# First input chunks loaded straight into a resident buffer, index scores that yield twice, and a norm's sums by operand, in a decoder trunk on one core

## The chip, the cores and the metric

The kernel runs on one core of one Trainium2 chip. The metric is the time of one execution in microseconds on the device, the median of several runs. Five engines of the core work side by side, each through its own list of instructions in order: TensorE (PE in the profile) for matmuls and transposes, VectorE (DVE), ScalarE (ACT), GpSimd (POOL), and SyncE (SP), which here only issues transfers. PEld is the loading of weights into TensorE's array, which overlaps its matmuls. Transfers between HBM and the on-chip memory go through DMA engines; an engine's row with a q behind its name (SPq, POOLq) is that engine issuing one.

## The reference

A trunk of two layers over 1024 tokens of width 1024, all in float32. Cut to what matters:

```python
for i in range(2):
    a = rmsnorm(h, norm_mix_pre[i])
    q, k, v, qi, ki, wi, u_conv, u_pool = split(a @ w_in[i])
    # partial rotary on q, k, qi, ki
    # dsa_sparse_attention, per block of 128 tokens:
    #   idx = sum over 16 index heads of relu(qi . ki) * wi; the top 256 causal keys are kept
    #   softmax attention of 8 heads over these keys
    mix = concatenate([attention, conformer_conv(u_conv), multiscale_pool(u_pool)])
    h = h + rmsnorm(mix @ w_out[i], norm_mix_post[i])
    m = square(relu(rmsnorm(h, norm_mlp_pre[i]) @ w_up[i])) @ w_down[i]
    h = h + rmsnorm(m, norm_mlp_post[i])
    h = h + sigmoid(h @ ple_gate[i]) * (p[i] @ ple_proj[i])
# rmsnorm(x, g) = x / sqrt(mean(x^2) + 1e-6) * g
```

## The kernel before

The tokens are cut in two halves of 512. A tensor is kept transposed, features on the 128 partitions and 512 tokens along them, so a half of width 1024 is eight chunks of 128 x 512. Every dense product is a chain of *units*: a unit takes one block of 128 output features, eight input chunks, and three matmuls for each of them (L252, L257, L258), because each number is split into a rounded high part and a low remainder and the product low times low is left out. That is 24 matmuls of 128 x 512 into one bank `pd` of a ring of three. `prepare` (L205) loads a unit's weights (512 KB, L208, issued by SP into a ring of two buffers `wraw`), rounds them on ScalarE (`whi`, L213) and subtracts on GpSimd (`wlo`, L214). The input chunks are split likewise by `split_g`: ScalarE L274 rounds, VectorE L275 subtracts; the two parts lie in a ring of 16 `slots`.

An RMS norm runs in three steps. `Sq.add` squares each chunk on ScalarE (L290) and adds it up on VectorE (L294); the last square is kept apart, so a norm has two operands. `token_sums` multiplies them with a column of ones (L307), so that four columns hold the sums of 4 x 128 tokens. `rms` scales them (VectorE L318), takes the power -1/2 (GpSimd L320), and `spread` brings the result back along the partitions (L312). In the input projection the norm's factor `rb` (ScalarE L327) is multiplied in as the units are evacuated.

The work goes in eight phases: the input projection (`win`) and the rest (`m`) of each layer and half, in the order of PHASES. A `win` phase has 21 units: six for the conv and pooling groups, and 15 for attention, among them I0 to I7, the index queries, whose results `put` rounds (L269), subtracts (L270) and writes to HBM (`qiS`, L364), and V, whose blocks are transposed by TensorE (L451). The first half's input is loaded by `first_x` ahead of everything, the second half's by a second call that is made at the 16th unit of the first phase. A chunk of x is loaded into a buffer `dtmp` (L1053), split, squared, and the buffer is given back. The ring `dtmp` has nine buffers, and almost every step between a bank and HBM uses it. `yT`, a resident 8 x 128 x 1024 buffer, holds the trunk's state between phases; until the first `m` phase nothing is in it.

The conv, pooling and attention stages are generators that run beside the dense units: `run` gives them a budget for each unit of the phase, and `advance` takes one step of the first generator in the list that has one. A generator that yields None passes the turn to the next. `attention` first scores index queries against keys (`index`: `load_k`, then for each block and four heads `load_q`, issued by GpSimd into a ring of two `qst`, L617, then L610, relu L651, sum L655), then selects, then does softmax and the weighted sum (transposes L798, products L806 and L807). What is left of an attention when its `m` phase begins is drained alone. Program order is only the start: a scheduler then reorders the instructions of each engine by its own estimate of times, and the rings decide who waits.

Of the kernel before, what the change touches and what calls it, by code (L numbers as in the profile page):

```python
# [16 lines left out]
OP = mybir.AluOpType  # L17

P = 128
# [4 lines left out]
NK = D // P  # L24
# [62 lines left out]
def tile_trunk(ctx: ExitStack, tc: tile.TileContext, xT, pT, pos, vecs, invf, cinv,  # L87
               win, wout, wup, wdown, wgate, wple, wcp, outT):
    nc = tc.nc
    te, ve, sc, gp, sy = nc.tensor, nc.vector, nc.scalar, nc.gpsimd, nc.sync  # L90
# [22 lines left out]
    qiS = dram.tile([2, 1024, S], F32, name="qiS")  # L113
# [12 lines left out]
    dtmp = Ring("dtmp", 9, [P, HALF])  # L126
# [10 lines left out]
    yT = const.tile([P, NK, HALF], F32, name="yT")  # L137
# [4 lines left out]
    def tiny(name, n=4, dt=F32, bufs=4):  # L142

        key = name + side[0][0]
        if key not in tinies:
            tinies[key] = [small.tile([P, n], dt, name=f"{key}{i}") for i in range(bufs)]
        tinies[key].append(tinies[key].pop(0))
        return tinies[key][-1]
# [11 lines left out]
    ones = const.tile([P, 1], F32, name="ones")  # L160
# [44 lines left out]
    def prepare(src):  # L205
        n = src.shape[1] // 4
        raw = wraw.get()
        sy.dma_start(raw[:, :4 * n], src)  # L208
        parts = []
        for i in range(n):  # L210
            hi, lo = whi.get(), wlo.get()
            r = raw[:, 4 * i:4 * i + 4]
            sc.activation(hi, r, AF.Copy)  # L213
            gp.tensor_tensor(lo, r, hi.bitcast(F32), op=OP.subtract)  # L214
            parts.append((hi, lo))
        wraw.put(raw)
        return parts
# [54 lines left out]
    def split_g(hi, lo, src, g):  # L272

        sc.activation(hi, src, AF.Identity, scale=g)  # L274
        ve.scalar_tensor_tensor(lo, src, g, hi.bitcast(F32), op0=OP.mult, op1=OP.subtract)  # L275


    class Sq:
# [20 lines left out]
        def rms(self, ps, other=None):  # L299
            rms(ps, self.acc, D, 1e-6, other)  # L300
            dtmp.put(*self.acc)

    def token_sums(ps, srcs):

        for j in range(4):
            for i, src in enumerate(srcs):
                te.matmul(ps[:, j:j + 1], src[:, j * P:(j + 1) * P], ones, start=i == 0, stop=i == len(srcs) - 1)  # L307

    def spread(ps, t4):

        for j in range(4):
            te.transpose(ps[:, j * P:(j + 1) * P], t4[:, j:j + 1].to_broadcast([P, P]), ident)  # L312

    def rms(ps, srcs, n, eps, other=None):

        token_sums(other or ps, srcs)
        v = tiny("rv")
        ve.tensor_scalar(v, (other or ps)[:, :4], 1.0 / n, eps, op0=OP.mult, op1=OP.add)  # L318
        r = tiny("rr")
        gp.tensor_tensor(r, v, mhalf, op=OP.pow)  # L320
        spread(ps, r)
# [146 lines left out]
    def conv_pool(l, hf, yc):  # L468
# [98 lines left out]
        ve.tensor_tensor(sq[0], sq[0], sq[1], op=OP.add)  # L567
        ctmp.put(sq.pop())
        rms(ps, sq, 256, 1e-5)
        ctmp.put(*sq)  # L570
        xs = []
# [24 lines left out]
    def attention(l, hf):  # L596
        blocks = list(range(4 * hf, 4 * hf + 4))
        sel = [b for b in blocks if (b + 1) * P > TOPK]
# [4 lines left out]
        def scores(q, W, k0):  # L603

            out = []
            for n0 in range(0, W, 512):
                n1 = min(W, n0 + 512)
                ps = banks.get()
                for k in range(2):
                    te.matmul(ps[:, :n1 - n0], q, kd[:, k, k0 + n0:k0 + n1], start=k == 0, stop=k == 1)  # L610
                out.append((n0, n1, ps))
            return out

        def load_q(src, b, h0, nh):
            x = qst.get()
            v = src.rearrange("k (d h) t -> (k d) h t", h=nh)
            gp.dma_start(x, v[:, h0:h0 + 4, b * P:(b + 1) * P])  # L617
            return x

        def load_k(h, k0, n):  # L620
            for dup in range(2):
                sy.dma_start(kd[dup * 64:(dup + 1) * 64, :, k0:k0 + n].bitcast(F32),
                             kS[l, :, :, :n].rearrange("k (d h) t -> h d k t", h=3)[h])
# [16 lines left out]
        def index():  # L640

            load_k(2, 0, Ws[-1])
            for j, b in enumerate(sel):
                W = Ws[j]
                for h in range(16):
                    if h % 4 == 0:
                        q = load_q(qiS, b, h, 16)
                    w = wiT[:, l, b, h:h + 1]
                    for n0, n1, ps in scores(q[:, h % 4], W, 0):
                        r, at = ps[:, :n1 - n0], idx[j][:, n0:n1]  # L650
                        sc.activation(r, r, AF.Relu)  # L651
                        if h == 0:
                            sc.activation(at, r, AF.Copy, scale=w)
                        else:
                            ve.scalar_tensor_tensor(at, r, w, at, op0=OP.mult, op1=OP.add)  # L655
                        banks.put(ps)
                    if h % 4 == 3:
                        qst.put(q)
                    yield W * 1.32 / 1024
                gp.affine_select(idx[j][:, W - P:], idx[j][:, W - P:], pattern=[[-1, P]], compare_op=OP.is_ge,  # L660
                                 fill=LOW, base=0, channel_multiplier=1)
            state["index", l, hf] = True
# [161 lines left out]
        def attend(some, at, ring):  # L824
# [3 lines left out]
            for step in [(kv, b, g) for kv in range(2) for b in some for g in (0, 2)] + [None]:  # L828
# [21 lines left out]
                before = step, pr  # L850

        yield from index()
        if hf == 0:
            while ("q", l, hf) not in state:
# [192 lines left out]
    def first_x(hf):  # L1047
        ts = slice(hf * HALF, hf * HALF + HALF)
        sq = Sq()
        xs = []  # L1050
        for k in range(NK):
            h = dtmp.get()
            sy.dma_start(h, xT[k * P:(k + 1) * P, ts])  # L1053
            if k == 0 and hf == 0:
                ready.append(prepare(coming.pop(0)))
            x = slots.get()
            xs.append(x)
            split_g(x[:, 0], x[:, 1], h, vec[:, 0, V_MIX_PRE + k:V_MIX_PRE + k + 1])
            sq.add(h)
            dtmp.put(h)  # L1060
        return xs, sq


# [31 lines left out]
    def drain(l, hf):  # L1095

        while advance([x for x in bg if x[0] == (l, hf)]) is not None:
            pass

    state["x", 0, 0] = first_x(0)  # L1100
    for i, (l, hf, phase) in enumerate(PHASES):
        if phase == "win":
            extra = {}
            if i == 0:
                extra = {2: lambda: (sy.dma_start(fr, invf), rope_tables(0)), 5: lambda: rope_tables(1),
                         16: lambda: state.update({("x", 0, 1): first_x(1)})}
            run(win_phase(l, hf, *state["x", l, hf]), RATES[i], extra)
        else:
            drain(l, hf)
            run(m_phase(l, hf), RATES[i])  # L1110
# [62 lines left out]
```

## Time and profile before

| | us |
|---|---|
| median of 3 runs | 2802.93 (2802.38 to 2804.43) |
| the profiled execution | 2803.82 |
| its span, first to last instruction | 2802.1 |
| TensorE busy | 2701.1 (96%) |
| VectorE busy | 1698.4 (61%) |
| ScalarE busy | 1599.7 (57%) |
| GpSimd busy | 1372.7 (49%) |

All times of rows are microseconds from the start of the span unless marked ns. The granted clock (PEclk) is the TensorE clock that the throttle granted, as a share of full speed: 1.00 is 2.4 GHz and 0.50 is 1.2 GHz. In rows of waits "A <- B" says that A's engine was idle until B was done; DMA stands for a transfer.

### The profile page before, as it was taken

The page shows a single profiled execution, that of the slowest core. Times are in us where ns is not written, and L with a number is a line of the kernel's source. Part 1 is how long each engine was busy: PE and PEld are TensorE (multiplying, and loading weights), DVE is VectorE, ACT ScalarE, POOL GpSimd, SP SyncE. Part 2 cuts the span into 40 slices and gives each one's busy share as a digit, 9 for nine tenths or more (in the row PEclk, how much of TensorE's full clock was granted, in tenths as well). Part 3 has the DMA queues.
Part 4 walks back from the last instruction along what each step waited for, and adds up shares of the span by engine and source line. Part 5 has one row for each costly group of instructions (what it writes and reads, how often), then busy time and mean ns, then how long its engine had stood idle before and what let it go on. Part 6 is the DMA issues. An engine that isn't in the chain of part 4 may idle for free.

```text
span 2802.1 us, 37352 instructions
## 1 busy us (share of the span) xinstructions
PE 2701.1 (96%) x12512; PEld 2224.5 (79%) x12512; DVE 1698.4 (61%) x3399; ACT 1599.7 (57%) x3008; POOL 1372.7 (49%) x1085
## 2 busy tenths in 40 slices
PE   8889989999999999999999989999999999999998
PEld 6678877887888787788888778788878887788886
DVE  7869668678657868784422595676785561411123
ACT  5357668776766544685633434677757664533343
POOL 4655425444334674544344764444443346544446
PEclk9999999999999999999999999999999999999999
DMA  5677555432343566543333656533222354422223
GB/s 177 203 184 226 147 140 150 109 98 84 94 109 108 185 204 192 177 128 117 90 101 103 213 156 212 155 105 110 93 85 84 105 176 150 144 98 98 98 94 132
DMA packets 193425, 380.63 MB, mean 136 GB/s; under 512 B 17232, under 2 KB 76752, under 8 KB 193232
## 3 DMA queue, kind: packets, MB, share of 16 engines
q1 hardware_dynamic: 150992, 357.26, 39.8%
q0 software_dynamic: 42240, 20.98, 4.4%
q8 instruction: 99, 1.62, 0.2%
q14 instruction: 94, 0.77, 0.1%
HBM read 305.81 MB, written 72.35 MB: 135 GB/s over the span
## 4 chain that ended last, share of the span: by engine, by line
PE 78%; DVE 10%; DMA 5%; issue 2%; ACT 2%; POOL 1%; SPq 0%; POOLq 0%; ACTq 0%; DVEq 0%
PE pd L252 22%; PE pd L257 22%; PE pd L258 22%; PE bank L610 6%; PE bank L798 2%; DVE bank L549 2%; PE bank L807 1%; PE bank L806 1%; DMA wraw<-win 1%; DVE row L761 1%; DVE dtmp L884 1%; PE pd L255 1%; PE pd L307 1%; POOL wlo L214 1%; DVE dtmp L270 1%
## 5 line engine op out<-in xcount | busy, mean ns | idle before, releaser
L214 POOL TENSOR_TENSOR wlo<-wraw,whi 128x512 fp32r<-128x512 f32 x824 | 1097.4, 1336 | 1215.7 <-ACT whi L213 1147.0
L252 PE MATMUL pd<-slot,whi 128*128 128x512 f32 x3296 | 1305.6, 397 | 44.5 <-ACT whi L213 8.9
L258 PE MATMUL pd<-slot,wlo 128*128 128x512 f32 x3168 | 1245.4, 394 | 5.4 <-POOL wlo L214 5.1
L257 PE MATMUL pd<-slot,whi 128*128 128x512 f32 x3168 | 1245.8, 393 | 0.0
L213 ACT ACTIVATE whi<-wraw 128x512 fp32r<-128x512 f32 x824 | 512.8, 627 | 722.3 <-PE pd L257 520.2
L252 PEld LDWEIGHTS pd<-slot,whi 128*128 128x128 f32 x3296 | 625.1, 190 | 181.6 <-ACT whi L213 10.8
L258 PEld LDWEIGHTS pd<-slot,wlo 128*128 128x128 f32 x3168 | 600.1, 189 | 132.6 <-POOL wlo L214 9.2
L257 PEld LDWEIGHTS pd<-slot,whi 128*128 128x128 f32 x3168 | 600.6, 190 | 121.0 <-DVE slot L275 1.2
L610 PE MATMUL bank<-kd,qst 128*128 128x512 f32 (+3 forms) x1024 | 263.4, 361 | 15.6 <-DMA qst<-qiS 6.3
L655 DVE SCALAR_TENSOR_TENSOR idx<-bank,wiT,idx 128x512 f32<-128x512 f32 (+3 forms) x300 | 190.0, 652 | 89.1 <-ACT bank L651 80.8
L610 PEld LDWEIGHTS bank<-kd,qst 128*128 128x128 f32 x1024 | 181.2, 193 | 50.5 <-DMA qst<-qiS 7.2
L651 ACT ACTIVATE bank<-bank 128x512 f32<-128x512 f32 (+2 forms) x320 | 154.6, 506 | 71.5 <-PE bank L610 69.5
L1004 DVE TENSOR_TENSOR yT<-yT,pd 128x512 f32<-128x512 f32 x96 | 65.5, 684 | 203.7 <-PE pd L258 203.1
L990 DVE SCALAR_TENSOR_TENSOR pd<-pd,rb 128x512 f32<-128x512 f32 x112 | 78.0, 696 | 166.9 <-PE pd L258 166.6
L678 DVE TENSOR_SCALAR_CACHE_REDUCE row<-row,cc 128x640 f32<-128x640 uint16 (+1 forms) x124 | 133.5, 1078 | 63.4 <-ACT row L692 56.6
L549 DVE SCALAR_TENSOR_TENSOR bank<-win,vec,bank 128x512 f32<-128x512 f32 x232 | 165.5, 746 | 7.7 <-ACT bank L547 6.0
L776 DVE CUSTOM_DVE_ANT_0 row<-bank,idx 128x512 f32<-128x512 f32 (+3 forms) x160 | 91.7, 592 | 71.4 <-PE bank L610 50.4
L692 ACT ACTIVATE row<-row,cc 128x768 f32<-128x768 uint16 (+1 forms) x124 | 121.4, 982 | 22.9 <-DVE cc L698 20.5
L270 DVE TENSOR_TENSOR cmat<-bank,cmat 128x512 fp32r<-128x512 f32 (+1 forms) x160 | 98.3, 631 | 34.5 <-ACT cmat L269 30.9
L270 DVE TENSOR_TENSOR slot<-pd,slot 128x512 fp32r<-128x512 f32 x112 | 76.8, 687 | 52.8 <-ACT slot L269 52.5
L784 ACT ACTIVATE row<-row,nmc 128x384 f32<-128x384 f32 (+5 forms) x96 | 84.1, 877 | 36.0 <-DVE nmc L780 26.7
L269 ACT ACTIVATE cmat<-bank 128x512 fp32r<-128x512 f32 (+1 forms) x160 | 83.7, 546 | 26.4 <-PE bank L798 23.1
(216 smaller groups left out, 2724.1 us busy)
## 6 DMA issues: line engine op xcount, KB each, us to landing
wraw<-wup SPq DMA_DIRECT2D x128, 512.0 KB
wraw<-wdown SPq DMA_DIRECT2D x128, 512.0 KB
wraw<-win SPq DMA_DIRECT2D x84, 512.0 KB
qiS<-dtmp SPq DMA_DIRECT2D x64, 256.0 KB
slot<-mixS SPq DMA_DIRECT2D x32, 512.0 KB
wraw<-wgate SPq DMA_DIRECT2D x32, 512.0 KB
qst<-qiS POOLq DMA_DIRECT2D x48, 256.0 KB, 3.9
hS<-yT SPq DMA_DIRECT2D x48, 256.0 KB
```

The costliest lines, as they stand in the source:

```text
L213: sc.activation(hi, r, AF.Copy)
L214: gp.tensor_tensor(lo, r, hi.bitcast(F32), op=OP.subtract)
L252: te.matmul(ps, wh, xh, start=i == 0, stop=False)
L257: te.matmul(ps, wh, xl, start=False, stop=False)
L258: te.matmul(ps, wl, xh, start=False, stop=i == n - 1)
L270: ve.tensor_tensor(lo, src, hi.bitcast(F32), op=OP.subtract)
L549: ve.scalar_tensor_tensor(acc[:, c] if k == TAPS - 1 else pa, src, w, pa, op0=OP.mult, op1=OP.add)
L610: te.matmul(ps[:, :n1 - n0], q, kd[:, k, k0 + n0:k0 + n1], start=k == 0, stop=k == 1)
L651: sc.activation(r, r, AF.Relu)
L655: ve.scalar_tensor_tensor(at, r, w, at, op0=OP.mult, op1=OP.add)
L678: ve.tensor_scalar(flags[:, :Ws[j]], of[j], t, None, op0=op, op1=OP.add, accum_out=dst[:, j:j + 1])
L692: sc.activation(flags[:, :Ws[j]], of[j], AF.Sign, scale=-1.0, bias=c[:, j:j + 1], accum_out=cnt[:, j:j + 1])
```

## The change

There are three parts.

*The chunks of x.* `first_x` loads the eight chunks of a half straight into `yT[:, k]`, all ahead of the splits; splits and squares read yT, and no `dtmp` is taken for x. The first unit's weights are loaded behind the second chunk instead of the first.

*The index stage.* `index` issues the load of its first index queries and then yields None twice, ahead of any score.

*The norm's sums.* `token_sums` puts the sums of operand i into columns 4i to 4i + 3, each of them a matmul that starts and stops its own accumulation, one operand after the other. `rms` adds the second four columns by one more VectorE instruction where there are two operands.

```diff
     def token_sums(ps, srcs):

-        for j in range(4):
-            for i, src in enumerate(srcs):
-                te.matmul(ps[:, j:j + 1], src[:, j * P:(j + 1) * P], ones, start=i == 0, stop=i == len(srcs) - 1)
+        for i, src in enumerate(srcs):
+            for j in range(4):
+                te.matmul(ps[:, 4 * i + j:4 * i + j + 1], src[:, j * P:(j + 1) * P], ones, start=True, stop=True)
...
         token_sums(other or ps, srcs)
-        v = tiny("rv")
-        ve.tensor_scalar(v, (other or ps)[:, :4], 1.0 / n, eps, op0=OP.mult, op1=OP.add)
+        v, sums = tiny("rv"), other or ps
+        ve.tensor_scalar(v, sums[:, :4], 1.0 / n, eps, op0=OP.mult, op1=OP.add)
+        if len(srcs) == 2:
+            ve.scalar_tensor_tensor(v, sums[:, 4:8], 1.0 / n, v, op0=OP.mult, op1=OP.add)
         r = tiny("rr")
...
         def index():

             load_k(2, 0, Ws[-1])
+            first = load_q(qiS, sel[0], 0, 16)
+            for _ in range(2):
+                yield None
             for j, b in enumerate(sel):
                 W = Ws[j]
                 for h in range(16):
                     if h % 4 == 0:
-                        q = load_q(qiS, b, h, 16)
+                        q = first if j == h == 0 else load_q(qiS, b, h, 16)
...
         for k in range(NK):
-            h = dtmp.get()
+            h = yT[:, k]
             sy.dma_start(h, xT[k * P:(k + 1) * P, ts])
-            if k == 0 and hf == 0:
+            if k == 1 and hf == 0:
                 ready.append(prepare(coming.pop(0)))
+        for k in range(NK):
+            h = yT[:, k]
             x = slots.get()
             xs.append(x)
             split_g(x[:, 0], x[:, 1], h, vec[:, 0, V_MIX_PRE + k:V_MIX_PRE + k + 1])
             sq.add(h)
-            dtmp.put(h)
         return xs, sq
```

The numbers of instructions on TensorE, ScalarE, GpSimd and SyncE stay as they are; VectorE has twelve more, one for each norm with two operands. Line numbers grow by two to six. Three places show how the order moves.

On SyncE, the part of the list where the last index queries (qiS) of the first phase are written. Before, with the second half's loads of x (xT) among the writes:

```order
L208 DMA wraw_92<-win 128x1024
L1053 DMA dtmp_106<-xT 128x512
L364 DMA qiS<-dtmp_103 128x512
L364 DMA qiS<-dtmp_102 128x512
L1053 DMA dtmp_102<-xT 128x512
L208 DMA wraw_91<-win 128x1024
L364 DMA qiS<-dtmp_107 128x512
L364 DMA qiS<-dtmp_101 128x512
L1053 DMA dtmp_101<-xT 128x512
```

And now the same writes:

```order
L208 DMA wraw_92<-win 128x1024
L366 DMA qiS<-dtmp_102 128x512
L366 DMA qiS<-dtmp_101 128x512
L208 DMA wraw_91<-win 128x1024
L366 DMA qiS<-dtmp_107 128x512
L366 DMA qiS<-dtmp_103 128x512
L208 DMA wraw_92<-win 128x1024
L366 DMA qiS<-dtmp_104 128x512
```

All sixteen loads of x have moved to the first fifteen rows of this engine; between the writes only weights are left.

On ScalarE, the rows that end with the first norm's factor (rb). Before:

```order
L290 ACTIVATE dtmp_108<-dtmp_109 128x512
L213 ACTIVATE whi_95<-wraw_92 128x512
L213 ACTIVATE whi_94<-wraw_91 128x512
L213 ACTIVATE whi_96<-wraw_92 128x512
L197 ACT_TABLE_LOAD
L197 ACTIVATE dtmp_105<-dtmp_101 128x512
L199 ACTIVATE dtmp_104<-dtmp_101 128x512
L327 ACTIVATE rb_164<-pd_137 128x512
```

And now:

```order
L274 ACTIVATE slot_86<-yT,vec 128x512
L274 ACTIVATE slot_87<-yT,vec 128x512
L274 ACTIVATE slot_88<-yT,vec 128x512
L274 ACTIVATE slot_89<-yT,vec 128x512
L274 ACTIVATE slot_90<-yT,vec 128x512
L213 ACTIVATE whi_95<-wraw_92 128x512
L213 ACTIVATE whi_96<-wraw_92 128x512
L329 ACTIVATE rb_164<-pd_137 128x512
```

The second half's roundings (slots 83 to 90) stand ahead of the factor now, and so do the weights of the unit that is fourth in line; the sine table of the positions has moved behind it.

On TensorE, the place where the first index scores (L610 before, L612 now) and the transposes of V (L451, now L453) stand, behind the last dense unit that they follow. Before:

```order
L258 MATMUL pd_137<-slot_82,wlo_98 128x512
L610 MATMUL bank_144<-kd,qst_128 128x384 x2
L610 MATMUL bank_140<-kd,qst_128 128x384 x2
L610 MATMUL bank_141<-kd,qst_128 128x384 x2
L610 MATMUL bank_142<-kd,qst_128 128x384 x2
L610 MATMUL bank_143<-kd,qst_129 128x384 x2
L451 MATMUL pd_138<-ident,dtmp_106 128x128 x4
L252 MATMUL pd_139<-slot_75,whi_93 128x512
```

And now:

```order
L258 MATMUL pd_137<-slot_82,wlo_98 128x512
L453 MATMUL pd_138<-ident,dtmp_109 128x128 x4
L252 MATMUL pd_139<-slot_75,whi_93 128x512
L257 MATMUL pd_139<-slot_75,whi_93 128x512
L612 MATMUL bank_144<-kd,qst_128 128x384 x2
L612 MATMUL bank_140<-kd,qst_128 128x384 x2
L612 MATMUL bank_141<-kd,qst_128 128x384 x2
L612 MATMUL bank_142<-kd,qst_128 128x384 x2
```

Four transposes and two dense matmuls now stand ahead of the first scores.

## Rows read from the trace of the kernel before

**Rows 1.** The page's first part: busy us, share of the span, instructions.

```profile
PE 2701.1 (96%) x12512; PEld 2224.5 (79%) x12512; DVE 1698.4 (61%) x3399; ACT 1599.7 (57%) x3008; POOL 1372.7 (49%) x1085
```

**Rows 2.** Stretches: length, busy us by engine (instructions), granted clock, DMA share, GB/s.

```profile
core 0: us, PE busy (x) PEld busy (x) DVE busy (x) ACT busy (x) POOL busy (x), PEclk, DMA share, GB/s
20.00:25.00 5.00, 5.00 (x31) 4.41 (x30) 4.93 (x9) 0.63 (x1) 2.20 (x1) 1.00 0.23 85
25.00:30.00 5.00, 1.78 (x7) 0.90 (x5) 4.15 (x10) 3.34 (x5) 2.52 (x2) 0.59 0.04 14
30.00:35.00 5.00, 4.21 (x10) 3.34 (x11) 4.68 (x7) 3.21 (x5) 1.91 (x2) 0.50 0.87 297
31.00:80.00 49.00, 46.98 (x196) 37.72 (x196) 44.45 (x63) 23.98 (x38) 26.91 (x22) 0.95 0.49 159
80.00:103.00 23.00, 17.31 (x59) 12.93 (x60) 22.62 (x35) 6.75 (x13) 13.36 (x10) 0.78 0.69 193
134.00:157.00 23.00, 12.77 (x46) 10.35 (x45) 10.62 (x18) 12.09 (x23) 9.19 (x8) 0.78 0.64 182
345.00:380.00 35.00, 26.76 (x127) 20.20 (x126) 22.51 (x56) 26.41 (x58) 4.83 (x5) 0.87 0.63 148
```

**Rows 3.** Waits from 100 to 160 us: total us, times, longest.

```profile
ACT slot L274 <- DMA dtmp<-xT: 13.9, 6, 4.1
...
PE pd L252 <- DVE dtmp L270: 3.9, 1, 3.9
...
ACT dtmp L290 <- DMA qiS<-dtmp: 2.4, 2, 1.2
```

**Rows 4.** The chain that ends at 158 us, in order: start, us, what.

```profile
119.12 3.48 DMA qiS<-dtmp
...
122.62 3.40 DMA dtmp<-xT
...
130.44 5.71 DMA dtmp<-xT
...
136.18 0.72 ACT slot L274
...
138.65 6.16 DMA qiS<-dtmp
...
145.58 6.65 DMA qst<-qiS
...
152.28 3.52 PE bank L610 x10
155.80 0.44 PE pd L451 x4
```

**Rows 5.** VectorE's timeline at the start: start, us, instruction, [idle before, releaser].

```profile
10.14 0.75 DVE L275 SCALAR_TENSOR_TENSOR slot<-dtmp,vec,slot 128x512 fp32r<-128x512 f32 x1 [3.54 <-ACT slot L274]
...
16.64 1.78 DVE L275 SCALAR_TENSOR_TENSOR slot<-dtmp,vec,slot 128x512 fp32r<-128x512 f32 x1
...
27.25 0.15 DVE L318 TENSOR_SCALAR rvd<-pd 128x4 f32<-128x4 f32 x1
...
30.28 0.49 DVE L191 TENSOR_SCALAR dtmp<-dtmp,fr 128x512 f32<-128x512 f32 x1 [1.03 <-ACT dtmp L199]
...
32.38 0.68 DVE L397 SCALAR_TENSOR_TENSOR win<-pd,rb 128x512 f32<-128x512 f32 x1
```

**Rows 6.** TensorE's timeline at the start.

```profile
22.78 1.84 PE L307 MATMUL pd<-ones,dtmp 128*128 128x1 f32 x16
...
28.66 1.12 PE L312 MATMUL pd<-ident,rrd 128*128 128x128 f32 x4 [2.99 <-POOL rrd L320]
30.79 0.80 PE L252 MATMUL pd<-slot,whi 128*128 128x512 f32 x1 [1.01 <-ACT rb L327]
```

**Rows 7.** SyncE's issues at the start: start, us, line.

```profile
11.52 2.86 SPq L1053 DMA_DIRECT2D dtmp<-xT  x3
```

**Rows 8.** The drain of the first attention, a stretch as in rows 2.

```profile
348.60:379.00 30.40, 22.16 (x108) 16.40 (x106) 20.56 (x47) 23.14 (x51) 3.53 (x4) 0.86 0.63 144
```

**Rows 9.** Timeline of the last norm, GpSimd and TensorE.

```profile
2741.57 1.01 POOL L320 TENSOR_TENSOR rrn<-rvn,mhalf 128x4 f32<-128x4 f32 x1 [1.58 <-DVE rvn L318]
...
2744.01 0.60 PE L312 MATMUL pd<-ident,rrn 128*128 128x128 f32 x4
```

## The prediction, made before the changed kernel was run

> **What bounds the kernel now.** I read four views in this order: the page's busy shares, a table of stretches, the waits of one stretch with its chain, and timelines of single engines. TensorE is busy 2701.1 us of 2802.1 [rows 1], so all that can be won is in the stretches where it is not; the table [rows 2] finds them early. The reader should see three. At the start TensorE works 1.78 us of the five between 25 and 30, with a granted clock of 0.59, and at half clock (0.50) in the next five. From 80 to 103 it works 17.31 us of 23 while VectorE works 22.62, so VectorE sets that stretch. From 134 to 157 it works 12.77 of 23, and there VectorE works only 10.62 and ScalarE 12.09: no engine is full, so the waits are on transfers. A fourth, 345 to 380, is the drain of layer 0's first attention, 26.76 of 35. The change touches the first, the third and the fourth, and must pass through the second.
>
> In the third stretch the waits [rows 3] name the input twice over: ScalarE waits 13.9 us for chunks of x, and TensorE 3.9 us for a buffer that a rounding on VectorE (L270) writes late. The chain [rows 4] shows how these hang together. Buffers of the ring of nine pass from a write of index queries (qiS, 3.48 us) to a load of x (3.40), later to another load of x (5.71), then through ScalarE and VectorE to the last qiS write (6.16), to the load of the index queries (qst, 6.65), and only then TensorE's first scores start at 152.28. TensorE idles 10.2 us of the 23 (23 − 12.77): the 3.9 us, and nearly all the rest ahead of these scores.
>
> All sums are made against the profiled execution: its span is 2802.1 us, its own time 2803.8, so 1.7 us lie around the span. It is 0.9 us above the median of the runs, 2802.93, and I take 0.9 off at the end.
>
> **Part 1, the chunks of x go into yT.** Loads of x need no ring buffer any more. Sixteen loads and their splits are not fewer, but they stand elsewhere: all sixteen loads come in the first rows of SP's queue, and the second half's eight hi roundings (ScalarE) and eight lo subtractions (VectorE) move from the third stretch to the start. Only its eight squares stay behind.
>
> *At the start.* Three of the first eight loads are issued at 11.52 us now, because the ring of nine is empty [rows 7]; they will leave right behind the others. The sums of the norm, which run at 22.78, then come a few us sooner, and 24 dense matmuls stand between them and the spread (L312), where 4 did; so the 2.99 us that TensorE waits for the norm's power and the 1.01 us for the scale row [rows 6] can go: at most 4.0. Against it stand two things. The scale row now stands on ScalarE behind the roundings of unit 3's weights, and these behind 2 MB of x for the second half; but the queues carried 14 GB/s from 25 to 30 us and 85 in the five before [rows 2], so there is room. And VectorE gets 8 subtractions of 0.75 us [rows 5] = 6.0 us ahead of the first evacuation, which ran at 32.38 (L397). VectorE is nearly full there (4.93 and 4.15 of 5 [rows 2]). Some of its work moved the other way: from 10.14 to 32.38 it does seven splits, seven adds, about fourteen operations for the position tables; now it does fifteen splits, seven adds and ten of the others, and no longer waits. I count the first evacuation between 31.5 and 34. So the ends are −4.0 (both holes vanish, VectorE keeps up) and +5.0 (6.0 us less the 1.03 us it now idles [rows 5]). I take **−1.0**: TensorE is earlier by some 2 to 3 us, but VectorE, which is what the 80 to 103 stretch waits for, by little.
>
> *In the third stretch.* Both x legs leave the chain, 3.40 + 5.71 us. What stays in each place is a square that writes a ring buffer, so it waits for that buffer's qiS write to land. The last qiS write can be issued when its unit's rounding is done: 138.65 now. The split on ScalarE in front of that rounding (0.72) goes, and of the load's 5.71 us I count only 0.9, since the square that stays needs the buffer too; so I take 137.0. The write took 3.48 and 6.16 us in this chain, the load of qst 6.65; without eight 256 KB loads among them I take 4.5 each, nearer the lower value. With the 0.8 us from landing to issue (144.81 to 145.58) the scores start at 137.0 + 4.5 + 0.8 + 4.5 = 146.8, against 152.28: 5.5 us. TensorE also has the four transposes of V (0.44 [rows 4]) and two dense matmuls (at this stretch's mean of 12.77 / 46 = 0.28 [rows 2]) ahead of the scores now, 1.0 us of work done inside the hole. Sum **−6.5**. The ends: 0, if the squares and the scores wait as long for the qiS landings as they waited for x; and −10.2, both holes gone.
>
> **Part 2, the index stage yields twice before its scores.** The load of its first queries is issued in front of the yields, the scores in a later turn. Conv and pooling generators get those turns, and the scores of each attention lie some dense matmuls later. Three of four attentions end well before their own drain and can be late for nothing: **0**, ends −2 and +2. The first, (0, 0), is drained in the fourth stretch. In the order of TensorE's instructions, 134 instructions other than dense ones stand in that drain, where 106 do now: four more scores, 12 more transposes of probabilities, 12 more products with V. In the drain one of the 108 matmuls takes 30.40 / 108 = 0.281 us of time and 22.16 / 108 = 0.205 of TensorE [rows 8]. So 28 more cost 7.9 us there, and 5.7 us leave the dense stream that they stood in before: **+2**. The ends are 0 (the added work fills the drain's waits, 8.2 us of 30.4) and +7.9 (the stream before gains nothing).
>
> **Part 3, a norm's sums operand by operand.** The same matmuls with one column each, into eight columns in place of four, and one more VectorE operation of four columns, in twelve norms; such a one takes 0.15 us [rows 5]. Their cover is the dense matmuls between sums and spread: in the last norm the power is done at 2742.58 and the spread starts at 2744.01, a slack of 1.4 us [rows 9]. So **0**; uncovered it would be 12 × 0.15 = +1.8, and taking the accumulation apart can win no more than the fraction of a microsecond that the sums' order leaves: −1.
>
> **The sum.** −1.0 − 6.5 + 2 + 0 = −5.5 on 2803.8: 2798.3, less the 0.9 for the median: **2797.5 us**. Its own range, with neighbouring values of the two large terms, is 2793 to 2802. A measurement of this kernel can tell about 0.2%, 5.6 us; faster by more than that means under 2797.3, slower means over 2808.5. My forecast stands on the border.
>
> **The rivals.**
>
> *A. The landings take the place of x.* The squares wait for qiS writes in the very ring that the loads waited for, and the roundings of the next unit are queued behind them on ScalarE; two such waits, 2.4 us, are there already [rows 3]. If each write keeps its 6.16 us, the scores start near 152 as before, and −6.5 becomes 0: 2803.8 − 1.0 + 2 = 2804.8, for the median 2803.9, no change. Against it: those writes shared the queues with the x loads.
>
> [...]
>
> *B. Slower: VectorE's stretch.* The eight subtractions go from a stretch where VectorE has 12 us to spare (10.62 of 23) to one where it has none, ahead of the stretch that it sets (22.62 of 23). Subtractions may take longer still: one took 1.78 us [rows 5]. If the first evacuation is at 34 or later, everything to 103 us moves by about 6 us, the hole at 80 to 103 grows, and with the added scores at +2 and half of the third stretch's gain given away it comes to 2803.8 + 6 + 2 − 3 = 2808.8; with none of the gain 2811.8. I put 2809. For it: VectorE's share in [rows 2]. Against it: TensorE is ahead by then, and VectorE's own waits of the stretch from 31 to 80 (4.6 us of 49) shrink.
>
> *C. All of it is won.* Both holes of the third stretch close (−10.2), the start gives 4.0, the drain costs nothing: 2803.8 − 14.2 = 2789.6, for the median 2789. Half clock after each hole would go with them. Against it: a qiS write and a qst load in a row still last longer than the dense work that is left.
>
> *D. The change does not do what it says.* The loads would not be early if yT were still in use, or if the scheduler left them where they were; in the order of SP's queue they all stand before row 15, so I give it nothing.
>
> **How the numbers follow.** Forecast 0.45, A 0.25, B 0.17, C 0.13. Of the forecast's case some 60% lies under 2797.3 given that its −6.5 may as well be −8, the rest within 0.2%. Faster: 0.27 + 0.13 + 0.02 from A = 0.42. Slower: 0.15 from B and 0.03 from A with a long drain = 0.18. Same: 0.40. The range 2789 to 2809 leaves out half of C and half of B's tail.
>
> **What the new profile would show.** Right: ScalarE's 13.9 us for x gone; the sums of the first norm before 21 us and the first evacuation by 32; the scores' start, counted from the last index unit, some 5 us sooner; the drain some 2 us longer in TensorE's busy time; sums and spread of the last norm where they are. Wrong: squares that wait over 8 us for qiS in that stretch (rival A); a first evacuation after 34 and VectorE full to 103 with more waiting on TensorE (rival B); a drain of more than 35 us.

## The result: 0.56% slower, and the profile after

The changed kernel takes 2820.56 us (median of 7 runs, 2811.2 to 2826.32) against 2804.43 us of the kernel before beside it: a ratio of 1.0056, 95% interval 1.0039 to 1.0073. I had forecast 2797.5 us and a range up to 2809. The profiled execution is 2823.9 us, 20 us longer than that of before. One thing in the description ahead is wrong: yT is 512 tokens wide, not 1024; it holds one half. So the second half's chunk k can be loaded as soon as the first half's has been split and squared, which is still at the start.

The page of after, busy time by engine; TensorE's rose by 7.7 us, its idle time by 12:

```profile
PE 2708.8 (96%) x12512; PEld 2231.0 (79%) x12512; DVE 1699.8 (60%) x3411; ACT 1598.7 (57%) x3008; POOL 1373.9 (49%) x1085
```

Where the time went can be counted without any view: both kernels have 9960 dense matmuls (L252 to L258, the conv branch's products among them) in almost the same order of work, so the start of the n-th in one trace against that in the other tells how late the kernel is by then. The difference by stage, in us, profile against the profile of before ("whole" is the change; e18 is the whole change in a later batch; the others are experiments below). A stage in which nothing is changed scatters by 1 to 3 us, in a few places by 4.5, and two profiles of one program (e3 and e17) are 6 us apart in the stage to 6600; the profile of e17 is the longest of its six runs. So a single entry of a few us is read below only where several programs agree.

| dense matmuls, us in before | whole | e18 | e1 chunks | e8 held | e2 yields | e17 sums | e16 sums, yields | e9 first norm | e5 unread |
|---|---|---|---|---|---|---|---|---|---|
| to 294, 0 to 102: start, VectorE's stretch | +6.4 | +6.8 | +3.0 | -0.7 | -0.7 | +5.8 | +5.6 | +3.5 | -0.8 |
| to 600, to 203: index units | -6.5 | -5.3 | -6.7 | -2.8 | -0.9 | +2.7 | -0.2 | +1.3 | +0.1 |
| to 1080, to 336 | +3.7 | +1.5 | +0.1 | -0.3 | -1.4 | -0.9 | +0.9 | -0.7 | -0.3 |
| to 1130, to 383: drain | +6.1 | +4.3 | +6.5 | +2.4 | +0.8 | +4.4 | +4.5 | +4.5 | +0.2 |
| to 2994, to 944 | -0.1 | +0.1 | +8.1 | +8.8 | -0.3 | -0.2 | 0.0 | -0.7 | -0.4 |
| to 3240, to 1007: fifth norm | +10.2 | +11.0 | -0.9 | -0.8 | -0.3 | +6.7 | +7.0 | +0.9 | +0.6 |
| to 6600, to 1922 | +1.9 | +2.3 | -0.1 | -2.7 | +2.3 | +3.9 | +1.2 | -0.2 | -2.9 |
| to 7920, to 2312: last attention | -5.0 | -5.8 | -0.7 | +1.6 | -5.6 | +10.8 | -4.9 | +0.4 | +1.4 |
| to the end | +3.3 | -1.1 | +0.8 | -1.0 | +1.6 | +0.4 | -0.3 | +0.7 | +4.5 |

The stretches of after that answer to [rows 2, 8], columns as there:

```profile
25.00:30.00 5.00, 0.87 (x6) 0.52 (x5) 5.00 (x10) 1.35 (x3) 3.56 (x2) 0.94 0.16 61
30.00:35.00 5.00, 5.00 (x16) 4.01 (x17) 5.00 (x7) 2.06 (x3) 2.10 (x2) 0.72 0.36 108
31.00:80.00 49.00, 43.80 (x184) 35.16 (x183) 43.50 (x64) 25.05 (x40) 24.36 (x20) 0.95 0.44 141
80.00:109.00 29.00, 18.76 (x69) 14.17 (x68) 28.56 (x38) 8.13 (x14) 17.98 (x15) 0.86 0.61 187
134.00:157.00 23.00, 22.47 (x104) 18.64 (x104) 12.87 (x19) 10.45 (x21) 12.51 (x11) 1.00 0.76 235
```

The drain in after, between the same dense matmuls as in [rows 8]:

```profile
351.70:388.70 37.00, 27.02 (x136) 20.84 (x133) 25.22 (x66) 28.21 (x64) 4.29 (x5) 0.85 0.58 126
```

And the stretch from 80 to 109 in before:

```profile
80.00:109.00 29.00, 23.31 (x86) 17.86 (x86) 28.62 (x42) 9.81 (x18) 19.22 (x14) 0.82 0.70 204
```

The stretch from 134 to 157 is closed: TensorE works 22.47 us of 23, where it had 12.77. VectorE is full from 20 to 35 and, as before, from 80 to 109; TensorE works only 18.76 us of those 29, where it had 23.31. The drain takes 37.0 us with 136 matmuls, where it took 30.4 with 108. The chain behind the index queries in after (start, us, what):

```profile
134.56 3.29 DMA qiS<-dtmp
...
141.93 2.96 DMA qiS<-dtmp
...
145.59 3.84 DMA qst<-qiS
...
149.47 1.68 PE bank L612 x8
```

No load of x stands in it, and against [rows 4] the last write takes 2.96 us where it took 6.16, the load of the queries 3.84 where it took 6.65 (a write further ahead in this chain, at 123.21, took 4.47). The waits from 100 to 175 us (engine, line, what for: us, times, longest) show what became of [rows 3]:

```profile
PE bank L612 <- DVE idx L683: 3.2, 1, 3.2
...
ACT dtmp L290 <- DMA qiS<-dtmp: 1.3, 2, 1.0
...
PE bank L612 <- DMA qst<-qiS: 0.5, 1, 0.5
```

At the start, VectorE's and then TensorE's timeline of after, answering to [rows 5, 6]:

```profile
24.88 0.15 DVE L318 TENSOR_SCALAR rvd<-pd 128x4 f32<-128x4 f32 x1
24.95 0.74 DVE L275 SCALAR_TENSOR_TENSOR slot<-yT,vec,slot 128x512 fp32r<-128x512 f32 x1
25.61 0.68 DVE L195 SCALAR_TENSOR_TENSOR dtmp<-dtmp,dtmp 128x512 f32<-128x512 f32 x1
26.21 0.15 DVE L320 SCALAR_TENSOR_TENSOR rvd<-pd,rvd 128x4 f32<-128x4 f32 x1
...
33.96 0.68 DVE L399 SCALAR_TENSOR_TENSOR win<-pd,rb 128x512 f32<-128x512 f32 x1
```

```profile
28.56 0.65 PE L312 MATMUL pd<-ident,rrd 128*128 128x128 f32 x4 [3.44 <-POOL rrd L322]
29.89 0.79 PE L252 MATMUL pd<-slot,whi 128*128 128x512 f32 x1 [0.69 <-ACT rb L329]
```

The two VectorE operations of one norm (L318, L320) are 1.33 us apart, since a split and a table operation stand between them in VectorE's queue; the power waits for the second, and TensorE for the power, 3.44 us. The first evacuation comes at 33.96, 1.6 us later than before. The norm ahead of the second layer's first projection (the fifth with two operands) has a longer distance, 2.57 us, and more. Its last sums on TensorE and its first VectorE operation in before:

```profile
953.61 1.40 PE L307 MATMUL pd<-ones,dtmp 128*128 128x1 f32 x12
...
956.58 0.16 DVE L318 TENSOR_SCALAR rvd<-pd 128x4 f32<-128x4 f32 x1
```

The last sums, and then VectorE, in after:

```profile
962.15 0.95 PE L307 MATMUL pd<-ones,dtmp 128*128 128x1 f32 x8
...
968.28 0.14 DVE L318 TENSOR_SCALAR rvd<-pd 128x4 f32<-128x4 f32 x1
968.35 0.73 DVE L551 SCALAR_TENSOR_TENSOR bank<-win,vec,bank 128x512 f32<-128x512 f32 x1
969.12 0.91 DVE L270 TENSOR_TENSOR ctmp<-ctmp,ctmp 64x512 fp32r<-64x512 f32 x1
970.06 0.76 DVE L551 SCALAR_TENSOR_TENSOR bank<-win,vec,bank 128x512 f32<-128x512 f32 x1
970.85 0.16 DVE L320 SCALAR_TENSOR_TENSOR rvd<-pd,rvd 128x4 f32<-128x4 f32 x1
```

TensorE there, in before and in after:

```profile
959.74 0.60 PE L312 MATMUL pd<-ident,rrd 128*128 128x128 f32 x4
961.02 0.50 PE L252 MATMUL pd<-slot,whi 128*128 128x512 f32 x1 [0.69 <-ACT rb L327]
```

```profile
973.23 0.79 PE L252 MATMUL bank<-cmat,cmat 128*128 128x512 f32 x1 [5.21 <-ACT cmat L269]
973.82 1.05 PE L312 MATMUL pd<-ident,rrd 128*128 128x128 f32 x4
975.57 0.79 PE L252 MATMUL pd<-slot,whi 128*128 128x512 f32 x1 [0.69 <-ACT rb L329]
```

So the first operation itself runs 5.2 us after the last sum, where it ran 1.6 us after it, and the second 2.57 us behind it. A product of the conv branch has come to stand ahead of the spread and waits 5.21 us for its operand, which VectorE delays too; the power is done at 972.1, so the spread alone would have made TensorE wait some 4 us. TensorE's granted clock is half for 10.2 us from 971.5 on. Before, it had nothing to wait for there but 0.69 us.

### The profile page after: what moved, and what is told of

It is laid out like the page before. It is cut to its first block, busy times and chain, and to the rows that moved or that the text cites. A ratio compares the mean times of both kernels' runs of the same rounds, so it can differ in the third digit from the quotient of the medians.

```text
span 2822.1 us, 37361 instructions
## 1 busy us (share of the span) xinstructions
PE 2708.8 (96%) x12512; PEld 2231.0 (79%) x12512; DVE 1699.8 (60%) x3411; ACT 1598.7 (57%) x3008; POOL 1373.9 (49%) x1085
## 4 chain that ended last, share of the span: by engine, by line
PE 77%; DVE 13%; DMA 4%; issue 3%; ACT 2%; POOL 1%; SPq 0%; POOLq 0%; ACTq 0%; DVEq 0%
PE pd L252 22%; PE pd L258 21%; PE pd L257 21%; PE bank L612 6%; DVE bank L551 2%; PE bank L803 2%; DMA wraw<-win 1%; PE bank L811 1%; PE bank L812 1%; DVE dtmp L889 1%; DVE slot L275 1%; DVE dtmp L270 1%; POOL wlo L214 1%; PE pd L255 1%; DVE row L766 1%
## 5 line engine op out<-in xcount | busy, mean ns | idle before, releaser
L252 PE MATMUL pd<-slot,whi 128*128 128x512 f32 x3296 | 1307.5, 397 | 45.6 <-ACT whi L213 10.8
L258 PE MATMUL pd<-slot,wlo 128*128 128x512 f32 x3168 | 1246.1, 394 | 4.6 <-POOL wlo L214 4.3
L252 PEld LDWEIGHTS pd<-slot,whi 128*128 128x128 f32 x3296 | 627.1, 190 | 182.8 <-ACT whi L213 18.3
L258 PEld LDWEIGHTS pd<-slot,wlo 128*128 128x128 f32 x3168 | 601.8, 190 | 132.1 <-POOL wlo L214 8.5
L612 PE MATMUL bank<-kd,qst 128*128 128x512 f32 (+3 forms) x1024 | 262.2, 360 | 17.6 <-DVE mxc L781 10.4
L612 PEld LDWEIGHTS bank<-kd,qst 128*128 128x128 f32 x1024 | 178.2, 192 | 49.2 <-DVE mxc L781 12.2
L656 ACT ACTIVATE bank<-bank 128x512 f32<-128x512 f32 (+3 forms) x320 | 153.0, 507 | 77.7 <-PE bank L612 75.2
L683 DVE TENSOR_SCALAR_CACHE_REDUCE row<-row,cc 128x640 f32<-128x640 uint16 (+1 forms) x124 | 133.5, 1078 | 67.4 <-ACT row L697 60.6
L294 DVE TENSOR_TENSOR dtmp<-dtmp,pd 128x512 f32<-128x512 f32 x60 | 41.1, 685 | 98.1 <-ACT pd L290 97.8
```

What stands on the lines that cost most here:

```text
L252: te.matmul(ps, wh, xh, start=i == 0, stop=False)
L258: te.matmul(ps, wl, xh, start=False, stop=i == n - 1)
L683: ve.tensor_scalar(flags[:, :Ws[j]], of[j], t, None, op0=op, op1=OP.add, accum_out=dst[:, j:j + 1])
```

## The experiments

Each ratio is against runs of before in the same batch, in brackets its 95% interval. The theories: **N**, each norm pays for its second VectorE operation; **S**, the second half's eight subtractions at the start; **R** or **O**, a small edit gives other orders of instructions far behind it, and these cost; **D**, the chunks lose by reordered attention stages.

### The parts alone (one batch)

e1, the chunks of x alone. 

> The chunks of x into yT alone, norms and index stage as before. Theory N (the norm's second VectorE operation makes the loss): no loss here, -6 to +3 us against before; VectorE's stretch ends 5 to 8 us later near 103 us and 8 to 13 us come back by 160 us; no hole of 5 us at the norm near 960 us. Theory S (the eight subtractions moved into VectorE's full stretch make it): +6 to +12 us, most of it standing at 103 us and not given back. Theory R (any edit reshuffles the order and costs by chance): +5 us or more, at places that the edit does not touch.

e2, the yields alone. 

> The two yields and the early load of index queries alone. The order of TensorE's work differs from before only in the second layer's second attention, between some 1800 and 2310 us. Theory N: -5 to +2 us, all in that stretch, the first attention's drain as before. The prediction's own step (the drain near 350 us grows by 2 us through the yields): a longer drain, +2 us there. Theory R: +5 us or more.

e3, the sums and their second operation alone. 

> The sums operand by operand and the second VectorE operation alone. Theory N: +8 to +15 us; the second operation comes 1 us or more after the first in the first norm and 2 us or more in the norm near 960 us, TensorE idles 4 us or more ahead of that norm's spread, and TensorE is at half clock there for 6 us or more. Theory S: within 3 us of before. Theory R: some loss, but not at the norms.

These three edits are the parts of the diff, word for word. e4 leaves before's sums and adds only:

```diff
+        if len(srcs) == 2:
+            ve.tensor_scalar(v, v, 1.0, 0.0, op0=OP.mult, op1=OP.add)
         r = tiny("rr")
```

> Before's sums, and in each norm with two operands one more VectorE operation that multiplies by 1 and adds 0; nothing else changes. Theory N: +6 to +14 us with the same hole near 960 us, since three other operations stand between the two there as well. If instead the order of the sums on TensorE makes the loss: within 3 us of before. Theory S: within 3 us.

| | ratio |
|---|---|
| e1 chunks | 1.0040 (1.0026 to 1.0055) |
| e2 yields | 0.9999 (0.9988 to 1.0010) |
| e3 sums | 1.0105 (1.0090 to 1.0120) |
| e4 second operation | 1.0090 (1.0077 to 1.0103) |

So the norm part loses, and one added VectorE operation of 0.16 us in twelve norms loses nearly as much without the new order of the sums: 25 us for 2 us of work. The two don't lose at the same places, though. The hole that was expected of e4 near 960 us isn't there; its wait at that spread:

```profile
PE pd L312 <- POOL rrd L322: 1.2, 1, 1.2
```

In e4 the first operation runs 1.6 us after the last sum, as in before, and the second 2.2 us behind it. The stage to 3240 costs 1.9 to 3.6 us in the four kernels that only add the operation (e4, e10, e13, e14), and 6.7 to 11.0 us in the five that have the sums by operand (the change, e3, e16 to e18), all with the wait of 5.2 us. So at the fifth norm the order that comes with the new sums costs more than the operation. What that is worth in the whole time isn't settled: the intervals of e3 and e4 overlap. e1 loses 11 us, more than theory N allowed. e2's time can't be told from before's; its trace differs from 1720 us to the end of the last attention, where it gains 5.6 us, and the first attention's drain has its old length (31.3 us against 30.5, from the last dense matmul ahead of it to the first behind). The step that put 2 us there on the yields is wrong.

### Is it VectorE's work, or the order? (e5, e9 to e11, e13, e14)

e5 adds the same operation, with its result in a tile that nothing reads:

```diff
+        if len(srcs) == 2:
+            ve.tensor_scalar(tiny("rx"), v, 1.0, 0.0, op0=OP.mult, op1=OP.add)
```

> As e4, but the added VectorE operation writes a tile that nothing reads, so no power waits for it; its order on every engine is that of before with twelve rows more. Theory N (what costs is that the power waits for a second operation, and what the order makes of that): within 3 us of before. Rival (twelve operations more on VectorE cost by themselves): +8 us or more, as e4.

1.0007 (0.9997 to 1.0018). Twelve more operations cost nothing that can be told; the order of the rest is that of before. What costs is that the power waits for the operation, or what the scheduler makes of that; no run adds the dependence and keeps the old order, so these two are told apart only by place, in the following runs. With it in a single norm the scheduler's order changes for three of the twelve, the first, the fifth and the tenth, and for those also far behind the norm; in the traces e4's order on TensorE differs from before's in the stretches where that of e9, e10 or e11 does, and nowhere else. Each was run alone:

```diff
+        if len(srcs) == 2:
+            seen.append(1)
+            if len(seen) == 1:   # 5 in e10, 10 in e11, in (1, 5, 10) in e13
+                ve.tensor_scalar(v, v, 1.0, 0.0, op0=OP.mult, op1=OP.add)
```

> As e4, but the added VectorE operation (times 1, plus 0) stands in the first norm only; the order of all engines differs from before's between there and some 850 us. Theory O (the operation costs little where it stands, and the loss comes from orders of instructions that the scheduler makes anew behind it): 2 us at the first spread, the first attention's drain 4 to 6 us longer at 350 to 390 us, nothing behind 900 us; in all +4 to +8. Theory N (each norm pays for its own operation): within 2 us beyond the 2 us at the spread, drain unchanged; in all +1 to +3.

> The added operation only in the norm ahead of the second layer's first projection, near 960 us (the fifth with two operands). Nothing changes before some 940 us. Theory O and N alike: TensorE waits 2 to 5 us ahead of or behind this norm's spread; O has further losses of 1 to 4 us up to 1700 us, N none. O: +4 to +9; N: +2 to +4.

> The added operation only in the tenth norm with two operands, near 2270 us. Its own spread waits for nothing (there are dense matmuls ahead of it), so theory N: within 2 us of before. Theory O: the order of SyncE's loads of weights and ScalarE's roundings behind it is another one, TensorE waits 3 us or more for rounded weights near 2315 us and is at half clock for 6 us; in all +6 to +12.

e9: 1.0026 (1.0016 to 1.0035), one operation of 0.16 us for 7 us. VectorE and TensorE at the first norm, then the stretch of the drain (columns as in rows 2):

```profile
28.59 0.15 DVE L320 TENSOR_SCALAR rvd<-pd 128x4 f32<-128x4 f32 x1
...
29.33 0.16 DVE L324 TENSOR_SCALAR rvd<-rvd 128x4 f32<-128x4 f32 x1
```

```profile
30.80 1.12 PE L312 MATMUL pd<-ident,rrd 128*128 128x128 f32 x4 [4.95 <-POOL rrd L326]
32.88 0.79 PE L252 MATMUL pd<-slot,whi 128*128 128x512 f32 x1 [0.96 <-ACT rb L333]
```

```profile
352.20:387.60 35.40, 26.09 (x136) 19.84 (x134) 25.53 (x66) 28.32 (x64) 4.30 (x5) 0.88 0.61 140
```

The operation itself costs 2.1 us at the spread. Then, 320 us later and with no edit there, the drain takes 35.4 us with 136 matmuls where it took 30.4 with 108 [rows 8]. Between the last dense matmul ahead of the drain and the first behind it stand 134 others, where 106 did: 28 have moved from the dense units into the drain. The whole change, e3, e4 and all others with the operation in the first norm have the same 134, e1, e7 and e8 122, and all these have a longer drain (34.0 to 37.0 us); e2, e5, e6, e10 and e11 have 106 and the old one (30.0 to 31.2). Theory O holds here; N's own price, the 2.1 us, is there too, but it is the smaller part.

e10: 1.0014 (1.0004 to 1.0024). TensorE at the fifth norm:

```profile
957.69 0.65 PE L312 MATMUL pd<-ident,rrd 128*128 128x128 f32 x4 [1.90 <-POOL rrd L326]
960.20 0.80 PE L252 MATMUL bank<-cmat,cmat 128*128 128x512 f32 x1 [1.86 <-ACT cmat L269]
```

3.4 us are lost in the stage to the 3240th dense matmul, about as much as these waits; the 2 us behind it are within the scatter. The ratio, some 4 us, lies where the ranges of N and O meet.

e11: 1.0006 (0.9995 to 1.0018): not told apart from before, so its +6 to +12 did not come. Its trace does have the wait; ScalarE and TensorE near 2305:

```profile
2301.34 0.58 ACT L1030 ACTIVATE pd<-pd 128x512 f32<-128x512 f32 x1 [5.25 <-PE pd L258]
2305.81 1.15 ACT L213 ACTIVATE whi<-wraw 128x512 fp32r<-128x512 f32 x2 [3.88 <-DMA wraw<-wgate]
```

```profile
2306.49 0.50 PE L252 MATMUL pd<-slot,whi 128*128 128x512 f32 x1 [2.92 <-ACT whi L213]
```

It is 4.7 us later by the 7920th dense matmul, 1.0 of which it wins back. To see whether these three norms carry all of it:

> The added operation in the first, fifth and tenth norm only, the three whose addition changes the order of any engine. If these three carry e4's loss: +0.75 to +1.0% (the same as e4 beside it, within 4 us). If they only add up as e9, e10 and e11 did: +0.35 to +0.6%, and the other nine norms hold the rest.

> e4 once more, on the chip and beside the runs of e13. If its loss holds on this chip: +0.8 to +1.0%. If it was partly that chip's or that hour's: +0.4 to +0.7%, as the sum of e9 to e11.

e13: 1.0048 (1.0036 to 1.0060); e14 beside it: 1.0055 (1.0042 to 1.0069). The three norms carry it, as far as these intervals can tell, and the sum of the three alone, from another batch, is near it (0.26 + 0.14 + 0.06 = 0.46%). But e14 is e4's kernel, which lost 0.90% in the first batch. The first batch ran on one chip and this one on another; of the 8 us by which the medians' distance shrank, 4.7 are in the kernel before, which took 2802.79 us there and 2807.50 here, and 3.2 in e4's program. Why is not settled; so ratios of one batch are compared where there are such.

### The chunks (e6 to e8)

e6 loads only the first half's chunks into yT (`h = yT[:, k] if hf == 0 else dtmp.get()`), e7 only the second half's. e8 is e1 with one column of yT written late, ahead of the second half's loads:

```diff
+            if (l, hf, name) == (0, 0, "I2"):
+                sc.activation(yT[:, :, 0:1], ps[:, 0:NK].rearrange("p (k o) -> p k o", o=1), AF.Copy)
             pd.put(ps)
```

> Only the first half's chunks go into yT; the second half's go through the ring as before. Its order has as many other instructions in the first attention's drain as before, but in the next attention's stage (dense matmuls 2300 to 2640) it is placed as in e1. Theory D (e1 loses through reordered attention stages): drain within 2 us of before, 4 to 8 us lost at 700 to 880 us, in all +2 to +7. Theory S (the eight subtractions make e1's loss): within 3 us of before.

> Only the second half's chunks go into yT, so its eight subtractions stand at the start as in e1. Theory S: the whole loss of e1, +8 to +13. Theory D: VectorE's stretch late by some 5 us at 103 us and made good by 170 us, the drain 4 to 7 us longer since 23 other instructions have moved into it, the next attention's stage +2, in all +3 to +8.

> As e1, but a one-column write into yT from the unit of the third index query (I2) stands ahead of the second half's loads, so that they and their subtractions come near 105 us and not at the start. Theory S: the loss of e1 goes, -8 to 0 us against before. Theory D: 4 to 6 us better than e1 at 103 us, but the drain and the next attention's stage are ordered as in e1 and lose the same 13 us; in all +3 to +8.

e6: 1.0014 (1.0002 to 1.0025); e7: 1.0028 (1.0018 to 1.0038); e8: 1.0014 (1.0004 to 1.0023). The first evacuation and VectorE's stretch, first e1, then e8:

```profile
35.05 0.68 DVE L397 SCALAR_TENSOR_TENSOR win<-pd,rb 128x512 f32<-128x512 f32 x1
```

```profile
80.00:109.00 29.00, 20.65 (x75) 15.62 (x74) 28.59 (x41) 9.77 (x17) 18.26 (x15) 0.82 0.65 206
```

```profile
32.97 0.69 DVE L397 SCALAR_TENSOR_TENSOR win<-pd,rb 128x512 f32<-128x512 f32 x1 [0.19 <-ACT rb L327]
```

```profile
80.00:109.00 29.00, 21.42 (x82) 16.00 (x83) 28.15 (x42) 10.23 (x18) 19.11 (x15) 0.94 0.68 209
```

With the subtractions held back the stretch ends where it did (101.1 us, before 101.8; e1 104.9, e7 108.1), so S is right on that place. But what e1 loses there it gains back at the index units (-6.7), and e8 gains less (-2.8); what is left in both are the drain and the next attention (+8), where the order is another one. In time all three lie in D's ranges and outside S's, e7 by little: e6 4 us, e7 8, e8 4, each with some 3 us to either side. e8 isn't faster than before; whether it is better than e1 can't be said, since e1 ran in another batch, and e7, in the same one, is 0.14% above it with intervals that overlap.

### Combinations (e12, e15 to e18)

e12 is e8 with the yields, e15 the chunks with the yields, e16 the sums with the yields; e17 and e18 run the sums alone and the whole change side by side.

> e8 (chunks in yT, the second half's held back until the third index query) with the two yields, and before's sums: the change without its costliest part. If parts add up: +0.14% and -0.01%, so between -2 and +6 us against before. If the yields gain what one profile of e2 showed (4.6 us): -3 to +2.

> The change without the norm part. If parts add up: +0.40% - 0.01%, so +9 to +13 us. If the whole change's 0.56% is what is left of a larger loss, with the norm part costing on top: +0.3 to +0.45%.

> The change without the chunks. If parts add up: +1.04%. Theory O (the yields give the second layer's second attention another order, in which the tenth norm's second operation has nothing to push): some 10 to 15 us less than e3 between 2060 and 2310 us, in all +0.4 to +0.75%.

> e3 once more, beside the whole change on one chip. If e3's loss was larger through that chip, as e14's against e4 (0.55 against 0.90%): +0.55 to +0.75%; otherwise +0.95 to +1.1%.

> The whole change once more, beside e17. If the whole change is the norm part with the chunks' gain and the yields' removal of the tenth norm's loss in it: 0.1 to 0.4% less than e17 beside it. If losses add up: 0.1 to 0.4% more than e17.

| | ratio |
|---|---|
| e12 held, yields | 1.0004 (0.9994 to 1.0015) |
| e15 chunks, yields | 1.0015 (1.0004 to 1.0026) |
| e16 sums, yields | 1.0034 (1.0022 to 1.0046) |
| e17 sums | 1.0082 (1.0066 to 1.0098) |
| e18 whole | 1.0036 (1.0023 to 1.0049) |

Most of these missed what was expected. e12 lies in both of its ranges; e15 and e16 lose less than either of theirs, e17 lies between its two, and e18 gains a little more on e17 than the 0.1 to 0.4% expected. Parts don't add up. Each of the three programs that ran in two batches lost less in the later one (the whole change 0.56 and 0.36%, e3 and e17 1.05 and 0.82%, e4 and e14 0.90 and 0.55%), so no comparison across batches is firm.

Side by side, the norm part alone loses 0.82% and the whole change 0.36%: chunks and yields win back more than half of what the sums lose. The stage table says where. The yields: 6600 to 7920 is +10.8 us in e17, -4.9 in e16 and -5.8 in e18; with another order in the last attention the wait behind the tenth norm isn't there. The chunks: -5.3 against +2.7 at the index units. And a loss that two parts share is paid once: the drain is +4 to +6.5 in e1, e17 and e18 alike. No version beat before; e2, e5, e11 and e12 can't be told from it.

## Why the prediction was wrong

**The step that failed is part 3, "So 0".** Run alone, that part cost 1.05 and 0.82% (e3, e17), some 23 to 29 us, more than the whole loss. The step took the cover from the last norm, where 12 dense matmuls hide the second operation (there the pair is 0.20 us apart, and nothing moves). The cover of the first norm did not hold: 24 dense matmuls stand there now, as I had counted, and TensorE still waits 3.44 us. [rows 6] already had it waiting 2.99 us for that norm's power, and I used the row only for what the chunks might win. And the cost of an operation in a chain is not its 0.15 us but its place in VectorE's queue: 1.33 and 2.57 us behind the first one, in two stretches where VectorE is full. My upper end, 12 x 0.15 us, could not hold that. A large share of the loss was in no term at all: an order made by a scheduler changes 300 us behind the edit, which in e9 cost 4.5 us where the operation itself cost 2.1, and the new sums bring an order at the fifth norm that costs more than the operation there. How the loss divides between waits for the operation and new orders is shown for these places, not for the whole. (The prediction's own sum gives 2797.4, not 2797.5 us.)

**The second half's gap.** Right in place: -6.5 forecast, -6.5 in the table and -5.3 in e18. That the size fits is partly luck. The hole closed altogether, as rival C had it (0.5 us idle from 134 to 157, where it was 10.2): the last write and the load of queries took 2.96 and 3.84 us, not 4.5 each, and TensorE entered the stretch some 8 us later. Some of that was lost again close by, as in the 3.2 us that TensorE now waits for VectorE's work on the scores (L683). Rival A, with squares that wait for the landings, fell: 1.3 us of waits. Why the write that had taken 6.16 us took 2.96 is not shown. No load of x stood beside it, but the queues carried more while it ran, 257 GB/s against 181. The Trainium skill, "DMA: Bandwidth & Descriptors", section "Anatomy of one DMA — SWDGE (gpsimd) path", has a fit for transfers that GpSimd issues; by it 256 KB would take 2.6 us (an estimate from that page). The loads of the queries, which GpSimd issues, took 6.65 and 3.84 us in these chains: the trace is above that estimate both times, and it decides.

**The start.** The term of -1.0 us was mis-sized. The sums did come sooner (done at 19.5, before 24.6), but the first operation on them stood in VectorE's full queue and came only 2.4 us sooner (24.88, before 27.25), and the second 1.33 us behind it, so the spread began where it had (28.56, before 28.66). The first evacuation came at 33.96, at the edge of my 31.5 to 34, and TensorE's stretch ended 6.4 us late: rival B's mechanism. The chunks alone show 3.0 us there (e1), the norm part without them 5.6 and 5.8 (e16, e17); the two don't add up. B's 6 us at 103 us were nearly met, its account of the rest was not: it let the third stretch's gain be given away, while in fact the gain stayed, and the time was lost at the fifth norm and in the drain.

**The yields.** The drain's +2 us was forecast for the wrong reason, and too small. The count of 134 matmuls against 106 was right, but the first norm's operation puts them there (e9) and not the yields (e2 has 106); and the 5.7 us that were to leave the dense stream did not show: the stage ahead of the drain is +3.7 us in the profile and +1.5 in e18, the drain +6.1 and +4.3. My own sign of being wrong, a drain of more than 35 us, came: 37.0. Where I put 0 for the yields, in the last attention, all six profiles with yields (e12 and e15 too) show -4.9 to -5.8 us, but all of them also +1.2 to +7.8 in the stage before, where the yields already change the order, and e2's time did not move.

## What to carry to other kernels

Cost an operation that is added to a dependent chain by what stands ahead of it in its engine's queue at the place with the least cover, and look that place up for each of its copies: the busiest norm decides, not the last. Where a scheduler sets the order, compare the orders of the two kernels everywhere and not only at the edit; each place where the order flips is a term with both signs, and parts that flip the same place don't add up. And make the edit once without its dependence (e5): if that costs nothing, the work is not the cause.

## What was not expected of the hardware

In the profile of the changed kernel TensorE was at half clock in 20 stretches of 101.6 us together, in before in 15 of 81.6 (from the clock's record in both traces), 20 us more; at half speed that is, as an estimate, 10 us of the 20 lost, and TensorE's busy time grew by 7.7 us. But e18, the same program, had 15 stretches of 83.5 us and a busy time of 2701.4 us, both near those of before, and was still 13.8 us longer. So the clock can account for the difference between two runs of one program, and the loss itself doesn't need it: in e18 it is nearly all idle time of TensorE. And the same program, e4 and e14, lost 0.90% in one batch and 0.55% in another; nothing in these runs tells why.
